# Small inputs of a rotary embedding: nine DMAs on two engines, or one on each of the two

## The chip, the cores and the metric

One core of a Trainium2 chip. The metric is the device time of one execution in microseconds (us). All runs told of here are in the fast state with a granted clock of 1.0, so they may be compared. Times in a trace count from the start of the profiled span, which is some 2 us shorter than the device time (85.5 of 87.28 us in the profiled run of the kernel before).

## The reference

```python
# x: (8, 8, 1024, 64) float32, freqs: (32,) float32, positions: (1024,) integers
angles = np.outer(positions, freqs)
cos, sin = np.cos(angles), np.sin(angles)
x_first, x_second = x[..., :32], x[..., 32:]
out_first  = x_first * cos - x_second * sin
out_second = x_first * sin + x_second * cos
return np.concatenate([out_first, out_second], axis=-1)
```

## The kernel before

x is cut into eight tiles of 128 partitions. A partition holds 64 positions of one head, so partition p needs the positions of chunk p % 16. Positions arrive as 64-bit integers: each of the 128 rows is 512 B. The 32 frequencies are copied to all 128 partitions, 128 B each.

```python
C = 64; chunks = seq // C      # 16
group = P // chunks            # 8
ntiles = bh // group           # 8

pos_i = singles.tile([P, C, 1], positions.dtype)
for g in range(group):
    eng = nc.sync if g % 2 == 0 else nc.scalar
    eng.dma_start(out=pos_i[g * chunks:(g + 1) * chunks],
                  in_=bass.AP(tensor=positions.tensor, offset=positions.offset,
                              ap=[[C, chunks], [1, C], [1, 1]]))
fr = singles.tile([P, half], f32)
nc.scalar.dma_start(out=fr, in_=freqs[None, :].to_broadcast([P, half]))

for g in range(ntiles):        # eight loads, float32 to bf16, all issued at once on GpSimd
    xt = xpool.tile([P, C, d], bf16)
    nc.gpsimd.dma_start(out=xt..., in_=hbm(x, g))

# ... VectorE: pos_f, fturn, turns, rounding; ScalarE: sin_h, whole, cos_h ...
for g in range(ntiles):
    # ... six VectorE operations per tile: t1, t2, of, os_, of - t2, os_ + t1 ...
    nc.gpsimd.dma_start(out=hbm(out, g), in_=ot...)   # bf16 to float32, the same queue
```

## Time and profile before

87.09 us, median of 3 runs (87.08 to 87.15). What matters:

| | us |
|---|---|
| frequencies issued / first VectorE operation on them | 2.60 / 14.31 |
| first large VectorE operation (`turns`) starts | 14.53 |
| first store issued / landed | 31.86 / 49.61 |
| last store issued / landed | 77.27 / 83.76 |
| span | 85.5 |

The page of the profile gives busy shares in 40 equal slices of the span (9 is 90% or more), the rate of the DMA engines in GB/s, and the DMA queues with packets (the pieces that the DMA engines' work is recorded in), megabytes and share of time.

```profile
span 85.5 us, 146 instructions
...
DVE  0000002995599999999999999999999999990000
...
DMA  0799979999999999999999999999999999999990
GB/s 8 81 225 208 184 140 231 203 226 203 226 203 226 211 218 215 215 222 207 222 326 460 399 475 391 475 391 475 383 475 391 468 391 468 391 468 368 376 368 0
...
q0 software_dynamic: 2304, 25.17, 96.4%
...
```

VectorE (DVE) is idle for six slices, then busy to slice 36. The DMA strip is full from slice 3 nearly to the end, but for slice 6, and GpSimd's queue q0 takes 96.4% of the time of all sixteen DMA engines. In the stretch of loads the GB/s strip falls once, from 225 in slice 3 to 140 in slice 6 (up to 12.8 us). It doubles at slice 21 only because bytes are counted on the destination: a load writes 1 MB of bf16, a store 2 MB of float32.

The timeline has start, duration, engine (with q: its sequencer), line, operation, operands, and in brackets the idle time before and what ended it.

```profile
...
0.74 1.82 ACTq L51 DMA_DIRECT2D pos_i<-in_positions_dram  x4
0.74 1.76 SPq L51 DMA_DIRECT2D pos_i<-in_positions_dram  x4
...
1.25 4.37 POOL L62 DMA_DIRECT2D xt<-in_x_dram  x8 [0.81 <-PEq L129]
2.60 0.43 ACTq L56 DMA_DIRECT2D fr<-in_freqs_dram  x1
...
8.60 0.20 DVE L69 CAST pos_f<-pos_i 128x64 f32<-128x64 int32 x1 [7.73 <-DMA pos_i<-in_positions_dram]
14.31 0.18 DVE L71 TENSOR_SCALAR fturn<-fr 128x32 f32<-128x32 f32 x1 [5.52 <-DMA fr<-in_freqs_dram]
14.53 2.29 DVE L73 TENSOR_TENSOR turns<-pos_f,fturn 128x2048 f32<-128x2048 f32 x1
...
31.85 0.54 POOL L103 DMA_DIRECT2D out_dram<-ot  x1 [26.23 <-DVE ot L102]
```

The DMA view has each group of issues, the KB of one, and the median time from issue to landing.

```profile
...
out_dram<-ot POOLq DMA_DIRECT2D x8, 2048.0 KB, 13.2
xt<-in_x_dram POOLq DMA_DIRECT2D x8, 1024.0 KB, 24.4
pos_i<-in_positions_dram ACTq DMA_DIRECT2D x4, 8.0 KB, 3.2
pos_i<-in_positions_dram SPq DMA_DIRECT2D x4, 8.0 KB, 2.9
fr<-in_freqs_dram ACTq DMA_DIRECT2D x1, 16.0 KB, 11.7
```

Frequencies are issued last on ScalarE, at 2.60 us, and take 11.7 us for 16 KB. VectorE waits 5.5 us for them after its wait for positions. That looks like a critical start-up. The landings, read from the trace's records of semaphore updates by DMAs, say otherwise:

```
us, last of 16 engines    1     2     3     4     5     6     7     8
loads of x             9.41 15.45 20.38 25.22 30.05 34.91 39.84 44.70
stores of out         49.61 54.46 59.32 64.18 69.03 73.89 78.75 83.76
```

Loads and stores share a queue and land strictly one after the other, 4.86 us apart: 2 MB of float32 in 4.86 us are 432 GB/s. The first store waits 17.8 us, mostly for loads ahead of it. The one irregular step is 6.04 us between the first two loads.

### The profile page before, as it was taken

The numbers are of one execution on the slowest core, as the hardware profiler recorded it, in microseconds if no ns is written. First come the engines' busy times: TensorE is split into PE (matmuls) and PEld (weight loads), VectorE is DVE, ScalarE is ACT, GpSimd is POOL, SyncE is SP. The second block draws the span as 40 slices with busy tenths as digits, with TensorE's granted clock in tenths as the row PEclk, the third lists the DMA queues.
The fourth block names the chain that finished last, engine by engine and source line by source line (L and its number), as shares of the span: only waits on it lengthen the run. The fifth ranks groups of instructions, "written<-read, shape, count | busy, mean of one in ns | idle before, by whom it ended". The sixth has DMA issues, their size and how long they took to land.

```text
span 85.5 us, 146 instructions
## 1 busy us (share of the span) xinstructions
DVE 60.8 (71%) x54; ACT 7.0 (8%) x4; POOL 8.8 (10%) x20
## 2 busy tenths in 40 slices
DVE  0000002995599999999999999999999999990000
ACT  0500000004992000000000000000000000000000
POOL 5960000000000011020020020020020002002000
DMA  0799979999999999999999999999999999999990
GB/s 8 81 225 208 184 140 231 203 226 203 226 203 226 211 218 215 215 222 207 222 326 460 399 475 391 475 391 475 383 475 391 468 391 468 391 468 368 376 368 0
DMA packets 2704, 25.25 MB, mean 295 GB/s; under 512 B 528, under 2 KB 656, under 8 KB 656
## 3 DMA queue, kind: packets, MB, share of 16 engines
q0 software_dynamic: 2304, 25.17, 96.4%
q10 hardware_dynamic: 272, 0.05, 0.4%
q1 hardware_dynamic: 128, 0.03, 0.3%
HBM read 16.86 MB, written 16.78 MB: 393 GB/s over the span
## 4 chain that ended last, share of the span: by engine, by line
issue 75%; DMA 10%; POOL 4%; POOLq 1%; PEldq 0%
DMA xt<-in_x_dram 10%; POOL out_dram L103 4%; POOLq L129 1%; POOLq L103 0%; PEldq L129 0%
## 5 line engine op out<-in xcount | busy, mean ns | idle before, releaser
L103 POOL DMA_DIRECT2D out_dram<-ot x8 | 4.3, 533 | 67.9 <-DVE ot L102 67.9
L97 DVE TENSOR_TENSOR t<-xt,sin_h 128x2048 bf16<-128x2048 bf16 x8 | 9.8, 1228 | 2.0 <-ACT sin_h L82 2.0
L102 DVE TENSOR_TENSOR ot<-ot,t 128x2048 bf16<-128x2048 bf16 x8 | 9.8, 1231 | 0.0
L100 DVE TENSOR_TENSOR ot<-xt,cos_h 128x2048 bf16<-128x2048 bf16 x8 | 9.8, 1230 | 0.0
L101 DVE TENSOR_TENSOR ot<-ot,t 128x2048 bf16<-128x2048 bf16 x8 | 9.8, 1229 | 0.0
L98 DVE TENSOR_TENSOR t<-xt,sin_h 128x2048 bf16<-128x2048 bf16 x8 | 9.8, 1228 | 0.0
L99 DVE TENSOR_TENSOR ot<-xt,cos_h 128x2048 bf16<-128x2048 bf16 x8 | 9.8, 1228 | 0.0
L69 DVE CAST pos_f<-pos_i 128x64 f32<-128x64 int32 x1 | 0.2, 196 | 7.7 <-DMA pos_i<-in_positions_dram 7.7
L62 POOL DMA_DIRECT2D xt<-in_x_dram x8 | 4.4, 579 | 0.8 <-PEq L129 0.8
L71 DVE TENSOR_SCALAR fturn<-fr 128x32 f32<-128x32 f32 x1 | 0.2, 181 | 5.5 <-DMA fr<-in_freqs_dram 5.5
L82 ACT ACTIVATE sin_h<-turns 128x2048 bf16<-128x2048 f32 x1 | 1.9, 1909 | 16.1 <-DVE turns L79 16.1
L79 DVE TENSOR_TENSOR turns<-turns,whole 128x2048 f32<-128x2048 f32 x1 | 2.3, 2293 | 0.0
L73 DVE TENSOR_TENSOR turns<-pos_f,fturn 128x2048 f32<-128x2048 f32 x1 | 2.3, 2293 | 0.0
L85 ACT ACTIVATE cos_h<-whole,half_pi 128x2048 bf16<-128x2048 f32 x1 | 2.0, 2002 | 0.0
L84 ACT ACTIVATE whole<-turns 128x2048 f32<-128x2048 f32 x1 | 1.9, 1893 | 0.0
L82 ACT ACT_TABLE_LOAD x1 | 1.3, 1283 | 3.1 <-DMA pos_i<-in_positions_dram 3.1
L77 DVE TENSOR_SCALAR whole<-turns 128x2048 f32<-128x2048 f32 x1 | 1.2, 1227 | 0.0
L67 DVE MEMSET half_pi<- 128x1 f32 x1 | 0.1, 59 | 0.8 <-PEq L118 0.8
L118 POOL MEMSET const-float32-0.0<- 128x1 f32 x1 | 0.1, 99 | 0.2 <-issue 0.2
L118 POOL MEMSET const-bfloat16-1.0<- 128x1 bf16 x1 | 0.1, 102 | 0.0
L118 POOL MEMSET const-float32-1.0<- 128x1 f32 x1 | 0.1, 99 | 0.0
L118 POOL MEMSET const-uint8-127<- 128x1 uint8 x1 | 0.1, 99 | 0.0
## 6 DMA issues: line engine op xcount, KB each, us to landing
out_dram<-ot POOLq DMA_DIRECT2D x8, 2048.0 KB, 13.2
xt<-in_x_dram POOLq DMA_DIRECT2D x8, 1024.0 KB, 24.4
pos_i<-in_positions_dram ACTq DMA_DIRECT2D x4, 8.0 KB, 3.2
pos_i<-in_positions_dram SPq DMA_DIRECT2D x4, 8.0 KB, 2.9
fr<-in_freqs_dram ACTq DMA_DIRECT2D x1, 16.0 KB, 11.7
```

The source lines that it names most:

```text
L62: nc.gpsimd.dma_start(out=xt.rearrange("p c d -> p (c d)"), in_=hbm(x, g))
L73: nc.vector.tensor_mul(out=turns, in0=pos_f.to_broadcast([P, C, half]), in1=fturn.to_broadcast([P, C, half]))
L79: nc.vector.tensor_sub(out=turns, in0=turns, in1=whole)
L82: nc.scalar.activation(out=sin_h, in_=turns, func=Sin, scale=twopi)
L85: nc.scalar.activation(out=cos_h, in_=whole, func=Sin, scale=-twopi, bias=half_pi)
L97: v.tensor_mul(out=t1, in0=xf, in1=sin_h)
L98: v.tensor_mul(out=t2, in0=xs, in1=sin_h)
L99: v.tensor_mul(out=of, in0=xf, in1=cos_h)
L100: v.tensor_mul(out=os_, in0=xs, in1=cos_h)
L101: v.tensor_sub(out=of, in0=of, in1=t2)
L102: v.tensor_add(out=os_, in0=os_, in1=t1)
L103: nc.gpsimd.dma_start(out=hbm(out, g), in_=ot.rearrange("p c d -> p (c d)"))
```

## The change

The intent is to have the small inputs earlier, with fewer DMAs: positions by one DMA with an eightfold repeated source, frequencies no longer behind four others.

```diff
-    for g in range(group):
-        eng = nc.sync if g % 2 == 0 else nc.scalar
-        eng.dma_start(
-            out=pos_i[g * chunks:(g + 1) * chunks],
-            in_=bass.AP(tensor=positions.tensor, offset=positions.offset,
-                        ap=[[C, chunks], [1, C], [1, 1]]))
+    nc.sync.dma_start(
+        out=pos_i,
+        in_=bass.AP(tensor=positions.tensor, offset=positions.offset,
+                    ap=[[0, group], [C, chunks], [1, C]]))
     fr = singles.tile([P, half], f32)
     nc.scalar.dma_start(out=fr, in_=freqs[None, :].to_broadcast([P, half]))
```

## The prediction

> **What bounds the kernel now.** Two chains run side by side.
>
> VectorE: the timeline shows it idle until frequencies land (fturn starts at 14.31 us), then busy without a gap, save 2.0 us for ScalarE's sine, until 76.97 us. The last store is issued at 77.27. Read alone, this says that landing positions (cast at 8.60) and frequencies earlier wins up to ten microseconds.
>
> DMA: the strip says 9 from 2.6 us to 84 us. The trace's landing records show why: the eight loads land at 9.41, 15.45, 20.38, 25.22, 30.05, 34.91, 39.84 and 44.70 us, the stores at 49.61, 54.46, 59.32, 64.18, 69.03, 73.89, 78.75 and 83.76. All sixteen sit in GpSimd's one queue and land one after the other, 4.86 us apart. The first store, issued at 31.86, lands 17.8 us later, because the loads ahead of it aren't done. So this queue is the bound: 16 x 4.86 = 77.8 of 85.5 us. VectorE's chain is as long only at its end (last store issued 77.27, the one before lands 78.75).
>
> **What the change does.** Seven DMA issues go (0.37 to 0.44 us each on two sequencers). Frequencies are issued at about 0.74 instead of 2.60 us. Bytes stay the same: 128 packets of 512 B, 128 of 128 B. Before, frequencies took 11.7 us to land: their packets ran from 7.93 us on, eight to a DMA engine, each waiting for an 8 KB packet of x (0.62 us). This agrees with the Trainium skill, "DMA: Bandwidth & Descriptors", section "Queues, rings and completion order": an engine takes packets from its queues in turn. First packets of x come at 2.61 us, those of positions at 1.73. So most small packets should now pass before x fills the engines; the rest interleave. Positions' source now starts with a dimension of 8; by the same page's rule on how many engines a DMA gets, it should run on 8 engines, 16 packets each. I expect frequencies to land at 3 to 7 us, positions at 3 to 10 us, and VectorE's first large operation at 4 to 10 us instead of 14.5.
>
> **What of it counts.** VectorE's 4 to 10 us turn into waiting of stores in the queue: worth nothing. What counts is the disturbance of the x stream. The second load took 6.04 us instead of 4.86: 1.2 us lost while frequencies interleaved (the strip falls from 225 to 140 GB/s). Positions' late packets cost the first load about 0.2 us (65 ns per pair). The last store's 0.15 us over its pace goes too. At most 1.5 us can be won. Some small packets will still meet x, and the engines with 16 position packets may lose 0.5 us (estimate, 33 ns each). The first x packets took 1.2 to 1.6 us; I take this start-up as unchanged. Net gain: 0.9 us.
>
> **Prediction:** 86.2 us, 8 in 10 between 85.3 and 87.1. Faster by over 2% (below 85.35): 0.11. Within 2%: 0.86. Slower: 0.03.
>
> **What the profile would show.** Right: idle VectorE time before fturn nearly gone; first store issued at 22 to 28 us; stores' median from issue to landing up from 13.2 to 18 to 22 us; landings still 4.86 us apart, second load under 5.5 us after the first; last landing 0.3 to 1.5 us earlier. Wrong: stores that land much before 49 us, or loads and stores overlapping at a higher combined rate, would mean that VectorE was the bound and the gain is several us.
>
> **What would make it wrong.** Sixteen packets on each of eight engines that stall x more than estimated; slow descriptor generation for the three-dimensional position source, so that positions land after 14 us and VectorE becomes the bound; start-up of x delayed by a burst of 256 small packets.

## The result

The changed kernel takes 86.54 us (median of 4 runs, 86.43 to 86.79) against 87.09 us (4 runs, 87.04 to 87.15) for the kernel before. The ratio is 0.9941, 95% interval 0.9919 to 0.9963. A ratio here is the mean time of one kernel's fast runs over that of the other's in the same rounds, so it is not quite the ratio of the medians. A difference counts as faster or slower here from 2% on; by the interval the change is clear of noise, at about 0.6%.

The same strips of the changed kernel, with the queue of SyncE (q1) added:

```profile
span 84.2 us, 132 instructions
...
DVE  0069927999999999999999999999999910000000
...
DMA  0399999999999999999999999999999999999990
GB/s 2 60 210 214 214 218 218 214 214 214 214 222 210 218 218 210 218 218 214 210 342 405 459 405 467 381 490 381 482 389 467 405 451 420 428 443 405 467 373 0
...
q0 software_dynamic: 2304, 25.17, 97.2%
q1 hardware_dynamic: 136, 0.07, 0.3%
...
```

VectorE starts 9 us earlier and now ends in slice 33, where it ended in slice 36. The DMA strip still runs to slice 39. The dip in GB/s is gone.

The timeline of the changed kernel, the lines that answer to those before:

```profile
...
0.74 0.36 ACTq L54 DMA_DIRECT2D fr<-in_freqs_dram  x1
0.74 0.74 SPq L49 DMA_DIRECT2D pos_i<-in_positions_dram  x1
...
1.25 4.38 POOL L60 DMA_DIRECT2D xt<-in_x_dram  x8 [0.80 <-PEq L127]
4.93 0.20 DVE L67 CAST pos_f<-pos_i 128x64 f32<-128x64 int32 x1 [4.06 <-DMA pos_i<-in_positions_dram]
5.04 0.17 DVE L69 TENSOR_SCALAR fturn<-fr 128x32 f32<-128x32 f32 x1
5.25 2.29 DVE L71 TENSOR_TENSOR turns<-pos_f,fturn 128x2048 f32<-128x2048 f32 x1
...
22.57 0.54 POOL L101 DMA_DIRECT2D out_dram<-ot  x1 [16.94 <-DVE ot L100]
...
```

And its DMA view (for positions it gives no median: the trace records 9 semaphore updates for them, where the frequencies have 16):

```profile
...
out_dram<-ot POOLq DMA_DIRECT2D x8, 2048.0 KB, 21.7
xt<-in_x_dram POOLq DMA_DIRECT2D x8, 1024.0 KB, 23.6
...
fr<-in_freqs_dram ACTq DMA_DIRECT2D x1, 16.0 KB, 3.6
```

Frequencies land in 3.6 instead of 11.7 us. `turns` starts at 5.25 instead of 14.53 us, and the first store is issued at 22.57 instead of 31.86. But stores now take a median 21.7 us from issue to landing, up from 13.2. The landings show what became of nine microseconds:

```
us, last of 16 engines    1     2     3     4     5     6     7     8
loads of x             9.81 14.67 19.60 24.44 29.27 34.14 39.07 43.93
stores of out         48.82 53.68 58.55 63.41 68.26 73.12 77.99 82.83
```

The sum goes as follows. The first load lands 0.40 us later. The second load comes 4.87 instead of 6.04 us after the first: 1.17 us gained. Loads 3 to 8 together take 29.25 us in both kernels, and from the eighth load to the seventh store it is 34.05 and 34.06 us. The last store comes 4.85 instead of 5.01 us after the seventh: 0.16 us gained. Together the last landing is 0.93 us earlier. The two profiled runs differ by 0.85 us (87.28 and 86.43), the medians by 0.55: the profiled run of the kernel before lies above the four in its median (87.04 to 87.15), and that of the change is the fastest of its four.

### The profile page after: what moved, and what is told of

The parts are those of the page before. It is cut to its first block, busy times and chain, and to the rows that moved or that the text cites. A ratio compares the mean times of both kernels' runs of the same rounds, so it can differ in the third digit from the quotient of the medians.

```text
span 84.2 us, 132 instructions
## 1 busy us (share of the span) xinstructions
DVE 60.7 (72%) x54; ACT 7.0 (8%) x4; POOL 8.9 (11%) x20
## 4 chain that ended last, share of the span: by engine, by line
issue 65%; DMA 10%; POOL 4%; POOLq 1%; PEldq 0%
DMA xt<-in_x_dram 10%; POOL out_dram L101 4%; POOLq L127 1%; POOLq L101 0%; PEldq L127 0%
## 6 DMA issues: line engine op xcount, KB each, us to landing
out_dram<-ot POOLq DMA_DIRECT2D x8, 2048.0 KB, 21.7
```

## The experiments

The theory is that the queue of sixteen x transfers bounds the kernel, so small transfers count only by how much they disturb it. Its rivals: VectorE's start is what counts (A); fewer DMA issues are what counts (B). Each kernel ran beside the kernel before on the same chip; its medians there were 87.07 to 87.20 us.

| run | median us (n) | ratio to before, 95% interval | load 1 | load 2 | load 8 | last store |
|---|---|---|---|---|---|---|
| before (first profile) | 87.09 (4) | 1 | 9.41 | 15.45 | 44.70 | 83.76 |
| the change | 86.54 (4) | 0.9941 (0.9919 to 0.9963) | 9.81 | 14.67 | 43.93 | 82.83 |
| after_again | 86.56 (6) | 0.9935 (0.9914 to 0.9957) | 10.01 | 14.88 | 44.12 | 83.02 |
| fr_first | 86.41 (6) | 0.9915 (0.9899 to 0.9931) | 10.12 | 14.78 | 44.04 | 82.94 |
| pos_one_fr_late | 86.83 (5) | 0.9962 (0.9948 to 0.9975) | 9.66 | 15.27 | 44.52 | 83.42 |
| pos_16_engines | 86.42 (5) | 0.9917 (0.9903 to 0.9931) | 9.63 | 14.54 | 43.98 | 82.91 |
| no_small (wrong result) | 86.17 (4) | 0.9885 (0.9869 to 0.9901) | 9.30 | 14.15 | 43.91 | 82.80 |
| behind_load0 | 87.92 (6) | 1.0089 (1.0060 to 1.0118) | 9.39 | 15.74 | 44.97 | 83.85 |
| behind_load0_spread (wrong result) | 86.52 (4) | 0.9920 (0.9907 to 0.9934) | 9.49 | 14.37 | 43.96 | 82.87 |
| before_spread (wrong result) | 86.32 (5) | 0.9894 (0.9879 to 0.9909) | 9.64 | 14.54 | 43.79 | 82.80 |

The last four columns are landings in us. The other four runs delay stores or reorder transfers; their sections tell them.

### Is VectorE's start worth anything? vector_late_7 and vector_late_14

```diff
     nc.vector.tensor_sub(out=turns, in0=turns, in1=whole)
+    for _ in range(2):        # 4 in vector_late_14; the result stays the same
+        nc.vector.tensor_scalar(out=whole, in0=turns, scalar1=magic, scalar2=magic,
+                                op0=Alu.add, op1=Alu.subtract)
+        nc.vector.tensor_sub(out=turns, in0=turns, in1=whole)
```

> The changed kernel with VectorE's rounding and subtraction done three times instead of once (the result stays the same): VectorE and every store issue come 7.1 us later. Queue theory: in the changed kernel the last store is issued at 67.98 us and lands at 82.83, and a store with an empty queue takes 6.5 us, so there are 8.4 us of slack: time unchanged at 86.3 to 86.7. VectorE theory: 93.6.

> The same with five passes instead of one: 14.2 us later. Queue theory: the slack of 8.4 us is used up, the last store is issued at 82.2 us and lands 6.5 us later at 88.7: time 92.3, that is 5.8 us more than the changed kernel and not 14.2. VectorE theory: 100.7.

Measured: 86.40 us and 92.04 us. In vector_late_7 VectorE works 7.1 us more and every store is issued 7.2 us later, at no cost. Its last one:

```profile
...
75.15 0.53 POOL L105 DMA_DIRECT2D out_dram<-ot  x1 [6.28 <-DVE ot L104]
```

In vector_late_14 the stores come one by one as VectorE makes them. Its page and its last two issues on GpSimd:

```profile
...
DVE  0079999999928999999999999999999999993000
...
DMA  0699999999999999999999999999992891991990
GB/s 4 95 185 225 222 211 211 225 218 200 225 222 200 222 222 214 207 225 222 396 429 450 450 400 436 458 399 425 370 443 102 363 465 65 399 465 44 421 465 0
...
```

```profile
...
75.53 0.53 POOL L105 DMA_DIRECT2D out_dram<-ot  x1 [6.28 <-DVE ot L104]
82.34 0.53 POOL L105 DMA_DIRECT2D out_dram<-ot  x1 [6.28 <-DVE ot L104]
```

The DMA strip has holes near its end for the first time, and the last store lands at 88.83 us, 6.5 us after its issue. Rival A is refuted for this kernel, but for one small term: the changed kernel has some 8 us of slack on VectorE. The kernel before had none left at its very end: its last store, too, landed 6.5 us after its issue, and the engines finished it within 0.15 us of each other instead of 0.5 to 0.6, a sign that they had waited for it together. So the last store's 0.16 us are most likely what VectorE's earlier start is worth.

### Which half of the change does it? fr_first and pos_one_fr_late

fr_first keeps all nine DMAs and only moves the frequencies to the front:

```diff
     pos_i = singles.tile([P, C, 1], positions.dtype)
+    fr = singles.tile([P, half], f32)
+    nc.scalar.dma_start(out=fr, in_=freqs[None, :].to_broadcast([P, half]))
     for g in range(group):
         ...
-    fr = singles.tile([P, half], f32)
-    nc.scalar.dma_start(out=fr, in_=freqs[None, :].to_broadcast([P, half]))
```

> The kernel before with one edit: the frequencies are issued first on ScalarE, ahead of its four position DMAs; all nine DMAs stay. Queue theory (the sixteen x transfers in one queue bound the time, and the small transfers count only by how much they disturb them): frequencies land by about 4 us, the late positions at 7 to 9 us, the second load comes under 5.1 us after the first instead of 6.04, time 86.3 to 86.8, so most of the gain of the change, although VectorE starts 3 to 4 us later than in the changed kernel. Rival A (VectorE's start is what counts): the time lies 3 to 4 us above that of the changed kernel, or at least in proportion to VectorE's start. Rival B (nine issues against two is what counts): no gain, 87.1.

Measured: 86.41 us, ratio 0.9915. Part of its timeline:

```profile
...
0.74 0.39 ACTq L50 DMA_DIRECT2D fr<-in_freqs_dram  x1
...
10.78 0.20 DVE L69 CAST pos_f<-pos_i 128x64 f32<-128x64 int32 x1 [5.68 <-DMA pos_i<-in_positions_dram]
11.01 2.29 DVE L73 TENSOR_TENSOR turns<-pos_f,fturn 128x2048 f32<-128x2048 f32 x1
...
```

Positions arrive so late that `turns` starts at 11.01 us, 5.8 us later than with the change, and the kernel is no slower for it. Nine issues are no handicap either. So B falls, and A once more. The Trainium skill says in "DMA: Bandwidth & Descriptors", section "Issuing engines are not separate DMA queues", that issuing from several engines only saves issue time; here even the number of issues is worth nothing measurable: 86.41 us with nine, 86.54 and 86.56 with two.

pos_one_fr_late is the other half. Positions come in one DMA, but a tiny activation holds the frequencies back:

```diff
     fr = singles.tile([P, half], f32)
+    warm = singles.tile([P, 1], f32)
+    nc.vector.memset(warm, 0.0)
+    nc.scalar.activation(out=fr[:, :1], in_=warm, func=Sin)
     nc.scalar.dma_start(out=fr, in_=freqs[None, :].to_broadcast([P, half]))
```

> The other half of the change alone: positions by one DMA on SyncE, but the frequencies are held back on ScalarE behind its table load and one tiny activation (which writes one column of the frequencies' tile first, so that the DMA has to wait for it), and issued at 2.3 to 2.6 us as in the kernel before (2.60). If the gain comes from frequencies passing ahead of x, it goes away: frequencies land at 7 to 12 us, the first two loads together take about 1.2 us longer than in the changed kernel (second load lands at 15.4 to 16.0 instead of 14.67), time 87.0 to 87.6, although there are only two small DMAs and VectorE still starts some us earlier than in the kernel before. If fewer issues or positions in one piece were the gain: 86.4 to 86.6.

Measured: 86.83 us, ratio 0.9962 (after_again, on the same chip in the same rounds: 0.9935). From its page and its timeline:

```profile
...
GB/s 0 127 197 196 138 199 220 209 224 205 228 201 232 201 232 197 232 201 232 201 340 402 464 402 464 402 464 402 464 394 471 402 440 425 425 440 417 440 379 0
...
```

```profile
...
2.27 0.36 ACTq L57 DMA_DIRECT2D fr<-in_freqs_dram  x1
3.13 0.20 DVE L70 CAST pos_f<-pos_i 128x64 f32<-128x64 int32 x1 [2.23 <-DMA pos_i<-in_positions_dram]
12.95 0.18 DVE L72 TENSOR_SCALAR fturn<-fr 128x32 f32<-128x32 f32 x1 [9.62 <-DMA fr<-in_freqs_dram]
...
```

The dip to 138 GB/s is back, one slice earlier than in the kernel before. The second load comes 5.61 us after the first: 0.75 us lost. The direction was as expected, but not the size. I expected 1.2 us and 87.0 to 87.6 us, and frequencies at 7 to 12 us; they landed at 12.85. Of a gain of 0.65% (after_again) 0.38% is left: the last landing is still 0.34 us earlier than before. Half of that is the last store's step, 4.84 instead of 5.01 us; the rest is the second load's smaller loss, less a later first load. Positions alone, without frequencies beside them, land at 3.11 us, before x fills the engines; in the changed kernel they landed at 4.91.

### All that the small transfers cost: no_small

```diff
-    nc.sync.dma_start(out=pos_i, in_=...)
+    nc.vector.memset(pos_i.bitcast(mybir.dt.int32), 0)
-    nc.scalar.dma_start(out=fr, in_=...)
+    nc.vector.memset(fr, 0.1)
```

> The changed kernel with positions and frequencies not loaded at all but set by memset on VectorE (a wrong result on purpose). It measures all that the small transfers cost. Queue theory: first packets of x at about 2.6 us and not delayed, first load lands at 8.7 to 9.3 us instead of 9.80, all others 4.86 apart, time 85.4 to 86.0; VectorE starts near 1.5 us and waits for x. Rival (x's slow start in the changed kernel is not due to the small packets): first load still at 9.6 to 9.9 us, time as the changed kernel, 86.5.

Measured: 86.17 us (wrong result), a little above the expected 85.4 to 86.0. The first load lands at 9.30, 0.5 to 0.7 us earlier than in the two profiles of the changed kernel. So the burst of small packets does delay x's start. The other profiles agree: the first load lands at 9.73 to 10.01 us in the six that start like the change (these two, vector_late_7, vector_late_14, loads_between_stores and pieces_alternate), and at 9.30 to 9.49 in the three without a small packet ahead of x (no_small and the two behind_load0 runs); the means are 0.44 us apart. About as much is lost again on the eighth load, which took 5.44 us instead of 4.86. In that stretch, at 41.0 to 42.8 us, 21 load packets took 0.68 to 1.06 us instead of 0.625. pos_16_engines and behind_load0_spread have 26 such packets each and eighth loads of 5.13 and 5.18 us, the change seven; before, fr_first and after_again have none there. I didn't find the cause.

### Does the number of DMA engines for positions matter? pos_16_engines

```diff
-        return bass.AP(..., ap=[[run, P], [1, run]])                       # x and out
+        return bass.AP(..., ap=[[run, chunks], [chunks * run, group], [1, run]])
-                    ap=[[0, group], [C, chunks], [1, C]]))                 # positions
+                    ap=[[C, chunks], [0, group], [1, C]]))
```

> The changed kernel, but partitions ordered chunk first and group second (x, out and positions alike), so that the positions' source has an outer dimension of 16 instead of 8. If the number of engines follows that dimension, positions now leave 16 semaphore packets instead of 8, 8 data packets on each engine, and they end about 0.3 us earlier; first load lands at 9.4 to 9.7 us instead of 9.80; time 86.1 to 86.5. If it doesn't follow it, nothing changes in the position packets. Risk: x's three-dimensional access costs GpSimd more per issue than 0.57 us, which would delay x's start.

Measured: 86.42 us. SyncE's queue in its page:

```profile
...
q1 hardware_dynamic: 144, 0.07, 0.3%
...
```

It has 144 packets, 128 of data and 16 of completion, where the changed kernel had 136: 128 and 8. This agrees with the Trainium skill, "DMA: Bandwidth & Descriptors", section "Why a DMA increments its semaphore by 16 and not by 1": the slowest dimensions of source and destination set the number of engines. Here the destination has 128 in both, and the source 8 or 16. Its first load lands at 9.63, against 9.81 and 10.01 with the change. The ratio, 0.9917 against 0.9941 and 0.9935, has an overlapping interval. A benefit is likely small and isn't shown.

### The small transfers in x's own queue: behind_load0

```diff
         xts.append(xt)
+        if g == 0:
+            nc.gpsimd.dma_start(out=pos_i, in_=...)      # sources as in the change
+            nc.gpsimd.dma_start(out=fr, in_=freqs[None, :].to_broadcast([P, half]))
```

> The changed kernel, but both small transfers are issued on GpSimd's own queue directly behind the first load of x. Queue theory: no burst ahead of x, so the first load lands at about 9.0 us; the small packets then pass in a row and cost the second load 0.2 to 0.6 us; VectorE starts at 9.5 to 10.5 us, 5 us later than in the changed kernel, at no cost; time 85.9 to 86.5. VectorE theory: about 5 us slower than the changed kernel, above 90.

Measured: 87.92 us, ratio 1.0089, slower than both kernels, and not because of VectorE: its `turns` starts at 11.12 us, as in fr_first. The strips, from its fastest run (87.52 us; what the slower ones lost besides isn't known):

```profile
...
DMA  0899999999999999999999999999999999999980
GB/s 0 92 211 203 113 215 207 223 207 223 211 219 211 219 211 223 207 223 211 223 303 438 430 438 415 445 430 430 438 422 438 438 422 438 422 445 415 445 330 0
...
```

The rate falls to 113 GB/s in one slice. The first load lands at 9.39, positions at 9.55, frequencies at 10.88, the second load at 15.74: 6.36 us for a 4.86 us transfer and 80 KB of small ones. I had expected 0.2 to 0.6 us for them and it is 1.5. Positions account for 0.17 of it. In GpSimd's queue the eight 128 B pieces that one DMA engine has form one packet of 1 KB; those sixteen packets took 1084 ns on average, while packets of 4 KB from positions beside them took 166 ns. Nothing takes turns with x here, so the taking of turns can't be the whole story of what frequencies cost.

### Is it the size of the pieces, or that all read the same 128 B? behind_load0_spread and before_spread

```diff
-            nc.gpsimd.dma_start(out=fr, in_=freqs[None, :].to_broadcast([P, half]))
+            nc.gpsimd.dma_start(out=fr, in_=bass.AP(tensor=x.tensor, offset=x.offset,
+                                                    ap=[[64, P], [1, half]]))
```

> behind_load0 (which lost: its second load came 6.36 us after the first, and its time was 87.92) with the frequencies' 128 reads of 128 B taken from 128 different places in x, 256 B apart, instead of 128 times from the same 128 B. A wrong result on purpose. If the size of the packets is what costs the x stream 1.3 us, the second load still comes 6.2 to 6.5 us after the first and the time is 87.5 to 88.3. If reading the same 128 B from all engines is what costs it, the second load comes 5.0 to 5.4 us after the first and the time is 86.4 to 87.0.

Measured (wrong result): the second load 4.88 us after the first, 86.52 us. From the packet records of the two traces:

```
the sixteen 1 KB packets of frequencies (8 x 128 B each)   mean ns of one
behind_load0           128 reads of the same 128 B                   1084
behind_load0_spread    128 reads, 256 B apart                          46
```

The same number, size and place in the queue, and the cost is gone.

On the page of behind_load0_spread the slice of 113 GB/s is gone:

```profile
...
GB/s 0 89 202 208 235 225 210 221 210 218 210 214 218 210 225 206 225 206 229 194 319 435 427 435 435 420 443 427 435 412 458 404 451 420 451 412 451 420 365 0
...
```

The same edit in the kernel before leaves all nine DMAs where they were:

> The kernel before with all nine small DMAs in their places, but the frequencies' 128 reads of 128 B taken from 128 different places in x instead of from the same 128 B. A wrong result on purpose. If what cost the second load 1.2 us is that all engines read the same 128 B (in behind_load0 such a packet took 1084 ns on average and 46 ns when spread), it goes away here too: the second load comes 4.85 to 5.1 us after the first instead of 6.04, VectorE starts up to 1 us earlier, last landing 0.5 to 1.4 us earlier, time 85.9 to 86.6, although the small packets still go between those of x and the frequencies still take over 8 us to land. If the taking of turns itself cost it, the second load stays at 5.8 to 6.1 us and the time at 87.0 to 87.2.

Measured (wrong result): 86.32 us, ratio 0.9894. Its page, without the dip to 140 GB/s, its timeline and its DMA view:

```profile
...
DMA  0799999999999999999999999999999999999990
GB/s 8 79 201 233 198 239 194 236 198 225 209 213 221 209 225 205 225 209 225 198 399 411 442 426 442 419 450 419 450 403 457 411 450 419 426 442 388 372 372 0
...
```

```profile
...
2.60 0.43 ACTq L56 DMA_DIRECT2D fr<-in_x_dram  x1
...
8.81 0.20 DVE L70 CAST pos_f<-pos_i 128x64 f32<-128x64 int32 x1 [7.94 <-DMA pos_i<-in_positions_dram]
13.35 0.18 DVE L72 TENSOR_SCALAR fturn<-fr 128x32 f32<-128x32 f32 x1 [4.34 <-DMA fr<-in_x_dram]
13.56 2.29 DVE L74 TENSOR_TENSOR turns<-pos_f,fturn 128x2048 f32<-128x2048 f32 x1
...
```

```profile
...
fr<-in_x_dram ACTq DMA_DIRECT2D x1, 16.0 KB, 10.7
```

The frequencies' packets still take turns with x's from 8.05 to 12.40 us and still need 10.7 us to land. Their last four rounds come about 0.61 us apart, in the kernel before about 0.85. VectorE starts at 13.56, only 1 us earlier than before. Yet the second load comes 4.90 us after the first, and the kernel is 1% faster. Between 9 and 13 us it starts 99 packets of x; the kernel before starts 79. In the kernel before, the records of the frequencies' own packets don't look slow (16 ns on average). The loss shows in x: of its packets started from 8 to 14 us, 30 took over 0.7 us there and none here, and the DMA strip there falls to 7 in slice 6. So the 1.2 us hang on where the 128 reads go, to one 128 B address among the frequencies or to 128 in x. The number and size of the small packets and their taking turns with x are the same in both.

### Could order or direction of the big transfers gain more? loads_between_stores and pieces_alternate

A load reads 2 MB and writes 1 MB, a store the reverse. If reading and writing overlapped between neighbours, alternating them would gain up to a quarter.

```diff
# loads_between_stores: only five loads are issued up front; then, behind each store
         nc.gpsimd.dma_start(out=hbm(out, g), in_=ot...)
+        if g + 5 < ntiles:
+            nc.gpsimd.dma_start(out=xts[g + 5]..., in_=hbm(x, g + 5))
# pieces_alternate: the same, store and load each cut into four pieces of 32 partitions
```

> The changed kernel with the last three loads of x issued not at the start but one behind each of the first three stores, so that loads and stores alternate in the queue. Queue theory, with each transfer costing an engine 4.86 us whatever its direction: same time as the changed kernel, 86.3 to 86.8, with landings still 4.86 us apart. Rival (a load is limited by reading and a store by writing, so neighbours overlap): landings closer than 4.7 us where loads and stores alternate, and a faster kernel by 1 us or more.

> As loads_between_stores, but stores and the last three loads cut into four pieces of 32 partitions each, two packets to an engine, so that directions alternate every two packets. Each transfer costs the same whatever its direction: 86.3 to 88 (more for the many issues and completions). If reading and writing overlap: the 26 transfers' worth of pieces that alternate run at up to 25 per cent less each, time 83 to 85.

Measured: 86.64 us and 88.81 us (ratios 0.9950 and 1.0212). The scheduler moved two of the three loads ahead again, so loads_between_stores has only one load between stores; its landings stay 4.84 to 5.05 us apart, the ones around that load 4.87. In pieces_alternate directions do alternate, and each quarter takes about 1.23 us, that is 4.9 us for a whole. Part of its loss may come from GpSimd waiting for earlier DMAs before an issue (mostly 0.5 to 1.3 us each time). I saw no overlap to be had in this form.

### The change once more: after_again

> The changed kernel once more, on the same chip as pos_one_fr_late, so that the two are compared directly: 86.4 to 86.7, ratio to the kernel before 0.992 to 0.995.

Measured: 86.56 us, ratio 0.9935. It repeats the first result (0.9941) and is the direct partner of pos_one_fr_late.

## Why the prediction was right

- **The queue bounds the kernel.** Right. Nine microseconds earlier on VectorE turned into waiting of stores (13.2 to 21.7 us), and vector_late_7 and vector_late_14 show the slack of about 8 us that follows: 7 us cost nothing, 14 us cost 5.5 us.
- **When the small inputs land.** Right: frequencies at 4.31 (3 to 7 expected), positions at 4.91 (3 to 10), the large operation at 5.25 (4 to 10), the first store at 22.57 (22 to 28). Positions ran on 8 engines, as the number of completion packets shows.
- **The second load's 1.2 us and the last store's 0.15 us.** Right in size: 1.17 and 0.16 us. Wrong in mechanism for the first. The prediction put it to frequencies interleaving with x. The interleaving sets when frequencies land, but before_spread has the same interleaving and loses nothing: its last rounds come 0.61 us apart, as the 0.62 us of the prediction has it, where the kernel before needed 0.85. The loss is gone when the 128 reads go to 128 places in x instead of one 128 B address.
- **Start-up of x "as unchanged".** This is the term that was mis-sized. I named a delay by the burst only as a risk, allowed for 0.5 us on the engines with 16 position packets, and expected 0.2 us back at the first load. It landed 0.40 us later in one profile and 0.60 in the other. no_small puts the whole delay by the small packets at 0.5 to 0.7 us, the nine profiles together at about 0.44. That the position engines are the cause isn't shown: with 8 packets on each (pos_16_engines) the first load still lands at 9.63.
- **The sum.** 0.9 us predicted; 0.93 at the last landing of the first profile and 0.74 in the second; 0.55 in the medians of the first comparison. The reading of the queue was right. That the landings fit so closely is partly luck: the 0.5 us allowed for one cause came as another's. About two fifths of the expected gain isn't seen in the first medians.

No correct kernel tried is clearly faster than the changed one. fr_first and pos_16_engines are level with it within their intervals, and no_small puts what is left in the small inputs at about half a per cent, or about one if its slow eighth load is an accident. Reading the frequencies once and copying them to the partitions on the chip was not tried.

It also stays open whether the loss comes from the address being the same or from where the frequencies lie, since the spread versions read from x; a run with 128 copies of the frequencies in their own tensor would tell. Positions, whose every row is read eight times, showed no such cost (166 ns for a packet of 4 KB in behind_load0).

## What to carry to other kernels

Before costing an earlier start of an idle engine, list the landings of the big transfers: if they follow one another at a fixed pace, only what breaks that pace counts. Look for the one irregular gap and ask what the DMA engines did in it. A tiny input copied to all partitions from one address can cost more of a saturated DMA stream than its bytes suggest, here 1.2 to 1.3 us for 16 KB. Issue it ahead of the stream: there both small inputs together delayed x by about 0.44 us.

## What the Trainium skill lacked or had wrong

- "DMA: Bandwidth & Descriptors", "Why small descriptors are slow (HBM only)", explains the cost by size alone. Missing: many reads of the same few bytes. Sixteen packets of 8 x 128 B took 1084 ns on average from one address and 46 ns from 128 addresses in another tensor; reads from the one address cost the stream of x 1.2 us (kernel before) and about 1.3 (behind_load0).
- The same page, "Rules for kernel authors", advises to coalesce many small transfers. Here one DMA for eight was not needed for the gain: nine DMAs in another order reached 0.9915 of the time, and one DMA for positions with late frequencies only 0.9962.
- The same page, "Where 436 GB/s comes from", says that the HBM side (about 358 GB/s) binds transfers between HBM and SBUF. In this one-core program the core moved 2 MB of float32 every 4.86 us, 432 GB/s, in loads and in stores. The page "HBM Reference", "Specifications (TRN2)", has it nearer, with about 425 GB/s for a core streaming alone.
- Found on no page: whether loads and stores in one GpSimd queue overlap. Alternating pieces still took 1.23 us a quarter, 4.9 us a whole, as in one direction.
